# Order of the first loads and of deferred steps in a hybrid attention and recurrence layer

## The chip, the cores and the metric

The kernel runs on one core of a Trainium2 chip. The metric is the device time of one execution in microseconds (us), the median of several runs. Engines: PE is the matrix engine, DVE the vector engine, ACT the scalar engine, POOL the general engine; SP issues the DMAs. A matmul's stationary operand is loaded first (PEld).

## The reference

One layer of a mixer. Context tokens (128) and latent tokens (1024), 1152 in all, each of width 1024, are normalised and modulated; one input projection gives six parts of width 1024 (queries, keys, values, the attention's gate, the recurrence's input and gate). Eight heads of differential attention and a bidirectional gated linear recurrence read the same normalised input.

```python
h = rms_norm(x, g_pre) * (1.0 + scale) + shift      # shift, scale, gate = split(silu(cond) @ w_ada + b_ada)
q, k, v, g_att, x_lru, g_lru = split(h @ w_in)
a = softmax(q1 k1) - lam * softmax(q2 k2)            # 8 heads; latents see context and latents
att = rms_norm(a @ v, g_subln) * (1 - lam_init) * silu(g_att)
u = centred_conv(x_lru); hf, hb = forward and backward linear scans of gated u
lru = (hf + hb) * silu(g_lru)
y = x + gate * rms_norm(concat(att, lru) @ w_out, g_post)   # also out: context keys, values, last states
```

## The kernel before

Everything is issued by hand in program order: each engine works its own queue in that order, and an instruction that waits holds up all that stands behind it on its engine. Products are split into high and low halves, so each needs three matmuls (`mm3`, line 118).

**First stage (lines 365 to 595).** Loads go out on SP in the order of the string in line 379: `A`, `B`, `C`, `D` are the four 512-column parts of the modulation matrix, each in four tiles of 512 KB (ring `wa` of 8, line 372); `x0` to `x7` are the transposed input, 576 KB each; `w` is a 512 KB block of the input projection. `mod(part, b)` (line 430) multiplies one modulation tile on PE; `mod_rows` copies the finished row off PSUM on ACT; `mod_turn` transposes it on PE and adds the bias on DVE; `scales`, `bounds` and `unit_h` turn it into the scale and shift of four x tiles. A and B serve x0 to x3, C and D serve x4 to x7; C and D accumulate in the PSUM banks of A and B. `sqsum(k)` squares a tile on ACT and adds it on DVE; nine small matmuls (line 521) sum over partitions, Newton steps give the reciprocal root on DVE, nine matmuls (line 529) spread it into `rb`. `normed(k)` multiplies a tile by `rb` (DVE), `modulate(k)` scales and shifts it and makes the high half `hTh` (ACT, or DVE for 6 and 7), `h_lo(k)` makes the low half (DVE). `w_square`, `w_unit`, `w_hi`, `w_lo` do the same for a weight block: square on ACT, sum on PE, power of two on DVE, high half on ACT, low half on DVE. `first_chunk(k)` and the loop in line 590 are the first real projection, tile by tile.

**Recurrence and projections (lines 621 to 1135).** A chunk (line 356) is 24 matmuls over 384 tokens, for values over 128 tokens; three chunks are one block of 128 columns, nine are a pair of value blocks. After each chunk of the second part, `tick()` (line 351) runs steps that were put off by `after(d, step)`. PSUM banks for chunks come from a ring of five (`small`, line 255), which the small matmuls (`un`, `wu`, `vmt`, `vmu`, `ktp`) share. The order of blocks is queries 0, 1, values 0, keys 0, 1, then for each further pair queries, queries, keys, keys, values, then the last two attention gates. A query or key block (`qk_block`, line 891) has the steps `squares` (ACT, sum of squares), `power` (PE sum `un`, DVE power of two), `turned` (rotary, four DVE operations), `halves` (ACT high, DVE low) and `send` (SP). A value block (`v_block`, line 960) has `peak`, `spread` (PE and DVE), `halves` and `send`. The recurrence's last block has its rest put off in the same way (lines 862 to 871).

**Attention (from line 1138)** starts with loads of keys, queries, the first output weights (`load_wo`, split on ACT and DVE or POOL) and a tile of the recurrence's result (`load_lt`).

## Time and profile before

| | before |
|---|---|
| median of three runs | 1272.1 us (1271.8 to 1272.23) |
| the profiled execution, its own time | 1273.15 us |
| its span | 1271.4 us |
| busy PE / DVE / ACT / POOL, share of the span | 90% / 82% / 62% / 24% |
| mean granted clock of PE | 0.967 of full |
| bytes moved by DMA | 188.77 MB |

The span is what the trace covers; the execution's own time holds 1.75 us more. Shares of busy time are averages over stages with different limits, so each stage is read by itself: a list of waits names who was late, a timeline shows the order on one engine, and a table of stretches gives the clock that PE was granted.

### The profile page before, as it was taken

The numbers are of one execution on the slowest core, as the hardware profiler recorded it, in microseconds if no ns is written. First come the engines' busy times: TensorE is split into PE (matmuls) and PEld (weight loads), VectorE is DVE, ScalarE is ACT, GpSimd is POOL, SyncE is SP. The second block draws the span as 40 slices with busy tenths as digits, with TensorE's granted clock in tenths as the row PEclk, the third lists the DMA queues.
The fourth block names the chain that finished last, engine by engine and source line by source line (L and its number), as shares of the span: only waits on it lengthen the run. The fifth ranks groups of instructions, "written<-read, shape, count | busy, mean of one in ns | idle before, by whom it ended". The sixth has DMA issues, their size and how long they took to land.

```text
span 1271.4 us, 20656 instructions
## 1 busy us (share of the span) xinstructions
PE 1145.8 (90%) x7804; PEld 791.4 (62%) x7804; DVE 1037.2 (82%) x1880; ACT 787.8 (62%) x1330; POOL 300.1 (24%) x172
## 2 busy tenths in 40 slices
PE   4879999999999789999899979988989888989886
PEld 1246666666666656675766747665666666666665
DVE  5686898889887878878868548899898989999976
ACT  4447577657766445645445347777877786777632
POOL 0000000000000000000000013345955586557724
PEclk8899999999999889999899989999999999999998
DMA  9311312231223244534433276999887998888864
GB/s 364 134 42 43 114 62 78 90 114 62 78 90 104 89 121 140 141 125 133 142 125 90 58 255 134 211 200 226 187 210 179 230 213 178 200 203 215 199 208 153
DMA packets 277820, 188.77 MB, mean 148 GB/s; under 512 B 196172, under 2 KB 246092, under 8 KB 276952
## 3 DMA queue, kind: packets, MB, share of 16 engines
q1 hardware_dynamic: 277432, 186.60, 54.2%
q8 instruction: 61, 1.00, 0.3%
q10 hardware_dynamic: 288, 0.85, 0.2%
q14 instruction: 39, 0.32, 0.1%
HBM read 102.20 MB, written 46.94 MB: 117 GB/s over the span
## 4 chain that ended last, share of the span: by engine, by line
DVE 38%; PE 34%; ACT 12%; issue 6%; DMA 5%; POOL 3%; SPq 1%; DVEq 0%; ACTq 0%; POOLq 0%
DVE mx L1228 6%; DVE e L1256 4%; DVE wlo L323 2%; PE ga L119 2%; DMA t<-a 2%; PE ga L120 2%; PE s L1219 2%; PE ga L121 2%; PE s L1221 2%; POOL a L1260 2%; ACT e L1238 2%; PE v L119 2%; PE v L121 2%; PE v L120 2%; PE x L119 1%
## 5 line engine op out<-in xcount | busy, mean ns | idle before, releaser
L1238 ACT ACTIVATE e<-s,mx,back 128x1152 f32<-128x1152 f32 (+1 forms) x144 | 175.5, 1218 | 68.7 <-DVE fa L1246 19.0
L1260 POOL TENSOR_TENSOR a<-e,a 128x1152 f16<-128x1152 f32 (+1 forms) x72 | 157.9, 2193 | 173.2 <-ACT a L1259 164.9
L113 POOL TENSOR_TENSOR wol<-wor,woh 128x512 fp32r<-128x512 f32 x24 | 33.7, 1406 | 692.3 <-ACT woh L222 692.3
L1228 DVE TENSOR_REDUCE mx<-s 128x1 f32<-128x1152 f32 (+1 forms) x144 | 177.3, 1231 | 22.1 <-PE s L1221 21.3
L119 PEld LDWEIGHTS <-whi 128*128 128x128 f16 x960 | 97.4, 101 | 64.2 <-issue 7.8
L121 PEld LDWEIGHTS <-wlo 128*128 128x128 f16 x960 | 94.2, 98 | 67.3 <-issue 5.7
L120 PEld LDWEIGHTS <-whi 128*128 128x128 f16 x960 | 94.3, 98 | 59.2 <-issue 3.1
L1219 PE MATMUL s<-kt,qt 128*128 128x384 f16 (+1 forms) x400 | 89.9, 330 | 45.7 <-ACT e L1238 43.3
L1256 DVE SCALAR_TENSOR_TENSOR e<-e,fa,e 128x1152 f32<-128x1152 f32 (+1 forms) x72 | 115.2, 1601 | 7.1 <-POOL ot L1306 0.5
L119 PE MATMUL po<-woh,lt 128*128 128x512 f32 x216 | 99.4, 460 | 9.6 <-DMA lt<-mix 4.6
L119 PE MATMUL pv<-vt,t 128*128 128x128 f16 x584 | 103.5, 221 | 4.9 <-DMA t<-a 2.7
L120 PE MATMUL pv<-vt,t 128*128 128x128 f16 x584 | 103.0, 221 | 0.0
L121 PE MATMUL pv<-vt,t 128*128 128x128 f16 x584 | 102.9, 221 | 0.0
L1259 ACT CAST a<-e 128x1152 f16<-128x1152 f32 (+1 forms) x72 | 75.8, 1053 | 40.9 <-DVE e L1256 25.8
L1221 PE MATMUL s<-kt,qt 128*128 128x384 f16 (+1 forms) x400 | 89.3, 329 | 0.0
L121 PE MATMUL po<-woh,lt 128*128 128x512 f32 x216 | 87.3, 404 | 0.0
L120 PE MATMUL po<-wol,lt 128*128 128x512 f32 x216 | 87.1, 403 | 0.0
L119 PE MATMUL v<-whi,hTh 128*128 128x256 f16 x288 | 81.9, 284 | 4.5 <-ACT qfq L759 3.4
L120 PE MATMUL v<-wlo,hTh 128*128 128x256 f16 x288 | 81.9, 285 | 0.0
L121 PE MATMUL v<-whi,hTl 128*128 128x256 f16 x288 | 81.9, 284 | 0.0
L1219 PEld LDWEIGHTS <-qt 128*128 128x128 f16 x400 | 34.1, 99 | 75.9 <-issue 63.4
L323 DVE SCALAR_TENSOR_TENSOR wlo<-wraw,wboth,whi 128x512 f16<-128x512 f32 x94 | 66.3, 747 | 18.3 <-ACT whi L313 18.3
(361 smaller groups left out, 3245.3 us busy)
## 6 DMA issues: line engine op xcount, KB each, us to landing
wraw<-in_w_in_dram SPq DMA_DIRECT2D x48, 512.0 KB, 3.5
lt<-mix SPq DMA_DIRECT2D x27, 512.0 KB, 3.9
qs<-hlq SPq DMA_DIRECT2D x64, 144.0 KB, 2.6
qt<-qs SPq DMA_DIRECT2D x72, 128.0 KB, 3.3
wa<-in_w_ada_dram SPq DMA_DIRECT2D x16, 512.0 KB, 8.9
wor<-in_w_out_dram SPq DMA_DIRECT2D x32, 256.0 KB, 4.1
mix<-amo SPq DMA_DIRECT2D x6, 1152.0 KB, 5.8
vs<-v SPq DMA_DIRECT2D x8, 640.0 KB, 3.0
```

The costliest lines, as they stand in the source:

```text
L113: eng.tensor_tensor(out=lo, in0=val, in1=f(hi), op=ALU.subtract)
L119: PE.matmul(out, lhsT=lh, rhs=rh, start=start, stop=False)
L120: PE.matmul(out, lhsT=lh, rhs=rl, start=False, stop=False)
L121: PE.matmul(out, lhsT=ll, rhs=rh, start=False, stop=stop)
L323: V.scalar_tensor_tensor(out=lo[:, i % 2, r], in0=raws[i][:, r], scalar=wboth[:, i, x:x + 1], in1=hi[:, i % 2, r], op0=ALU.mult, op1=ALU.s ...
L1219: PE.matmul(sps[:, j, :w_], lhsT=qt[:, mp], rhs=kt_[:, mp, c], start=True, stop=False)
L1221: PE.matmul(sps[:, j, :w_], lhsT=qt[:, 2 + mp], rhs=kt_[:, mp, c], start=False, stop=True)
L1228: V.tensor_reduce(out=d["mx"][:, mp:mp + 1], in_=sv, axis=AX.XY, op=ALU.max, negate=True)
L1238: S.activation(out=e_[:, :nk].rearrange("p (j c) -> p j c", c=w_), in_=sv, func=AF.Exp, bias=d["mx"][:, mp:mp + 1], scale=unit, accum_out= ...
L1256: V.scalar_tensor_tensor(out=e1, in0=e1, scalar=d["fa"], in1=e0, op0=ALU.mult, op1=ALU.subtract)
L1259: S.copy(out=a16[:, 0:nk], in_=e1)
L1260: G.tensor_tensor(out=a16[:, nk:2 * nk], in0=e1, in1=a16[:, 0:nk], op=ALU.subtract)
```

## The change

The loads of the first stage are put in turns of two x tiles and one B tile, and the matmuls, sums and small steps of that stage follow that order; C and D are multiplied earlier in the program, and two weight-block squares move. In the projection stage the scratch output of `squares` is no longer a tile of the ring `a` but the one scratch tile `wjunk`, made wider; `power` stands ahead of `turned` and one chunk earlier; the value steps come two chunks later for the first pair and one chunk earlier for the others; the recurrence's rest starts its roots one chunk later and all that follows too. At the start of attention `load_lt(0, 0)` is issued ahead of the four `load_wo`.

```diff
--- before.py
+++ after.py
@@ -274,7 +274,7 @@
         place = {x: i for i, x in enumerate(order)}
         raws, wts = {}, {}
         cnt = {"load": 0, "square": 0, "unit": 0, "cast": 0, "tick": 0}
-        junk = wp.tile([P, KT, P], mybir.dt.bfloat16, name="wjunk", bufs=1)
+        junk = wp.tile([P, T + CTX], mybir.dt.bfloat16, name="wjunk", bufs=1)
 
         def w_load():
             i = cnt["load"]
@@ -287,7 +287,8 @@
 
         def w_square():
             i = cnt["square"]
-            S.activation(out=junk, in_=raws[i], func=AF.Square, accum_out=wsq[:, i:i + 1])
+            S.activation(out=junk[:, :D].rearrange("p (k c) -> p k c", k=KT), in_=raws[i], func=AF.Square,
+                         accum_out=wsq[:, i:i + 1])
             cnt["square"] += 1
 
         def w_unit(bank=None):
@@ -376,7 +377,7 @@
 
             xt = [sp.tile([P, T], F32, name=f"xt{k}") for k in range(KT)]
             what = {"A": (0, 1), "B": (0, 0), "C": (1, 1), "D": (1, 0)}
-            for x in "A0 A1 w A2 A3 B0 B1 x0 x1 x2 x3 x4 x5 x6 x7 B2 B3 C0 C1 C2 C3 D0 D1 D2 D3 w w w".split():
+            for x in "A0 A1 w A2 A3 x0 x1 B0 x2 x3 B1 x4 x5 B2 x6 x7 B3 C0 C1 C2 C3 D0 D1 D2 D3 w w w".split():
                 if x == "w":
                     w_load()
                 elif x[0] == "x":
@@ -508,56 +509,61 @@
             for b in range(4):
                 mod(*A, b)
             w_square()
+            mod(*B, 0)
             w_unit(ssq)
             w_lo(w_hi())
-            for b in range(2):
-                mod(*B, b)
-            for k in range(KT):
+            for k in range(3):
                 sqsum(k)
-                if k == 2:
-                    mod_rows(*A)
+            mod_rows(*A)
+            mod(*B, 1)
+            for k in range(3, 5):
+                sqsum(k)
             mod_turn(*A)
+            mod(*B, 2)
+            for k in range(5, KT):
+                sqsum(k)
+            mod(*B, 3)
+            mod_rows(*B)
+            mod(*C, 0)
+            mod_turn(*B)
+            scales(0)
+            bounds(0)
             for t in range(NT):
                 PE.matmul(ssq[:, t:t + 1], lhsT=qsum[:, t * P:(t + 1) * P], rhs=onesf[:, 0:1], start=True, stop=True)
             V.tensor_scalar(out=xc, in0=ssq[:, :NT], scalar1=-0.5 / D, scalar2=-0.5 * EPS, op0=ALU.mult, op1=ALU.add)
             for k in NEWTON:
                 newton(k, xc, yc, tcol)
-            for b in range(2, 4):
-                mod(*B, b)
-            mod_rows(*B)
+            mod(*C, 1)
+            unit_h(0)
+            mod(*C, 2)
             for t in range(NT):
                 PE.matmul(rb[:, t // 3, (t % 3) * P:(t % 3 + 1) * P], lhsT=yc[:, t:t + 1].to_broadcast([P, P]), rhs=ident,
                           start=True, stop=True)
-            mod_turn(*B)
             normed(0)
-            scales(0)
-            bounds(0)
-            unit_h(0)
-            for b in range(2):
-                mod(*C, b)
             normed(1)
             modulate(0, S)
+            mod(*C, 3)
             modulate(1, S)
             normed(2)
             h_lo(0)
+            mod_rows(*C)
             normed(3)
-            for b in range(2, 4):
-                mod(*C, b)
+            mod(*D_, 0)
             modulate(2, S)
-            mod_rows(*C)
+            h_lo(1)
+            mod_turn(*C)
+            for b in range(1, 4):
+                mod(*D_, b)
+            normed(4)
             modulate(3, S)
-            h_lo(1)
-            normed(4)
-            mod_turn(*C)
-            for b in range(4):
-                mod(*D_, b)
-            mod_rows(*D_)
             h_lo(2)
             normed(5)
+            w_square()
+            mod_rows(*D_)
             h_lo(3)
             normed(6)
+            w_unit(ssq)
             normed(7)
-            w_square()
             accs = [small(f"x0_{j}") for j in range(NCH)]
             accb = big("x0b")
 
@@ -574,8 +580,6 @@
             shares()
             for k in range(2, 4):
                 first_chunk(k)
-            w_unit(ssq)
-            w_square()
             modulate(4, S)
             modulate(6, hi=V)
             h_lo(6)
@@ -590,6 +594,7 @@
             for x, k in enumerate((4, 6, 7, 5)):
                 for j in range(NCH):
                     chunk(accb[:, j], 16, 0, j, [k], x == 0, x == 3)
+            w_square()
             w_back(w_unit(ssq))
             w_square()
             w_ahead(0, ssq)
@@ -863,12 +868,13 @@
         decays(p)
         gated(p, 0)
         gated(p, 1)
-        after(1, lambda: (weights(p, 0), weights(p, 1), roots(p)))
-        after(2, lambda: (driven(p, 0), scan(p, 0)))
-        after(3, lambda: (driven(p, 1), scan(p, 1)))
-        after(4, lambda: (both(p), mixed(p)))
-        after(5, lambda: (mix_split(p), finish_state()))
-        after(6, lambda: mix_send(p))
+        after(1, lambda: (weights(p, 0), weights(p, 1)))
+        after(2, lambda: roots(p))
+        after(3, lambda: (driven(p, 0), scan(p, 0)))
+        after(4, lambda: (driven(p, 1), scan(p, 1)))
+        after(5, lambda: (both(p), mixed(p)))
+        after(6, lambda: (mix_split(p), finish_state()))
+        after(7, lambda: mix_send(p))
 
 
         cosT = lp.tile([P, LAT], F32, tag="uh", name="cosT", bufs=1)
@@ -898,7 +904,6 @@
 
             def squares():
                 d["sq"] = lp.tile([P, 1], F32, tag="qsq", name=f"sq{name}")
-                junk = lp.tile([P, T + CTX], F32, tag="a", name=f"j{name}")
                 S.activation(out=junk[:, :w_], in_=t_[:, :w_], func=AF.Square, accum_out=d["sq"])
 
             def context_keys():
@@ -941,7 +946,7 @@
             if which:
                 nc.sync.dma_start(out=t_[:, T:], in_=io["cache_kT"][:, h])
 
-            steps = [squares, turned, power, halves, send]
+            steps = [squares, power, turned, halves, send]
             if not first:
                 for j in range(NCH):
                     qk_chunk(which, h, t_, j)
@@ -950,11 +955,11 @@
                 squares()
                 if which:
                     after(1, context_keys)
-                for x, step in zip((1, 2, 3, 4), steps[1:]):
+                for x, step in zip((1, 1, 3, 4), steps[1:]):
                     after(x, step)
             else:
 
-                for x, step in zip(((6, 8, 9, 10, 11), (7, 10, 11, 12, 13))[h], steps):
+                for x, step in zip(((5, 7, 8, 10, 11), (7, 9, 10, 12, 13))[h], steps):
                     after(x - 3 * h, step)
 
         def v_block(pr):
@@ -1023,10 +1028,8 @@
                     nc.sync.dma_start(out=vs[pr][:, m], in_=d["v16"][m])
 
             d = {}
-            after(2, peak)
-            after(3, spread)
-            after(4, halves)
-            after(5, send)
+            for x, step in zip((1, 2, 3, 4) if pr else (4, 5, 6, 7), (peak, spread, halves, send)):
+                after(x, step)
 
 
 
@@ -1117,9 +1120,9 @@
             load_k(0, n)
         for n in range(2):
             load_q(n)
+        load_lt(0, 0)
         for kt in GROUPS[0]:
             load_wo(kt, 0)
-        load_lt(0, 0)
         after(2, lambda: [split_wo(kt, 0, V if kt % 2 else G) for kt in GROUPS[0][:2]])
         after(3, lambda: [split_wo(kt, 0, V if kt % 2 else G) for kt in GROUPS[0][2:]])
         after(3, lambda: [load_wo(kt, 1) for kt in GROUPS[0]])
```

## Rows read from the trace of the kernel before

**Rows 1.** table of stretches (stretch, length, busy us per engine, granted clock, DMA share, GB/s): projections

```profile
390.00:740.00 350.00, 325.90 (x2253) 225.55 (x2250) 260.91 (x587) 168.62 (x295) 0.00 (x0) 0.96 0.40 122
```

**Rows 2.** timeline of the first 40 us (start, length, engine, line, operation, tiles, count, [idle before])

```profile
5.62 8.62 PE L433 MATMUL modpA<-wa,cs 128*2 128x512 f32 x16 [5.62 <-DVE sp L406]
...
18.62 10.13 DVE L505 TENSOR_TENSOR qsum<-qsum,sq 128x1152 f32<-128x1152 f32 x7 [0.82 <-ACT sq L503]
...
28.89 4.00 PE L521 MATMUL ssq<-onesf,qsum 128*128 128x1 f32 x18 [8.30 <-DVE modT L445]
...
32.82 5.24 PE L433 MATMUL modpB<-wa,cs 128*2 128x512 f32 x8
...
37.98 2.27 PE L529 MATMUL rb<-ident,yc 128*128 128x128 f32 x18
```

**Rows 3.** the x tiles: issue of their loads and time to landing

```profile
L384 SPq DMA_DIRECT2D xt<-in_xT_dram x8: 328/328/467, 5.1 to 13.6; - x8
...
DMA to landing us min/median/max: 9.8/11.1/11.4
```

**Rows 4.** table of stretches as in rows 1: two stretches of the first stage

```profile
16.00:20.00 4.00, 2.07 (x5) 0.26 (x3) 2.64 (x2) 4.00 (x5) 0.00 (x0) 1.00 1.02 411
...
24.00:28.00 4.00, 0.00 (x0) 0.00 (x0) 3.69 (x4) 2.44 (x3) 0.00 (x0) 0.50 1.05 388
```

**Rows 5.** timeline from 40 to 90 us

```profile
40.71 1.34 DVE L482 TENSOR_TENSOR xt<-xt,rb 128x1152 f32<-128x1152 f32 x1
...
44.47 1.63 ACT L491 ACTIVATE xt<-xt,sh,sc 128x128 f32<-128x128 f32 x2 [5.81 <-DVE sh L470]
...
52.62 0.57 ACT L438 COPY rows<-modpA 2x512 f32<-2x512 f32 x1
...
53.57 7.03 PE L433 MATMUL modpB<-wa,cs 128*2 128x512 f32 x16
...
64.00 0.17 DVE L445 TENSOR_TENSOR modT<-ssq,vec 128x8 f32<-128x8 f32 x1 [3.82 <-PE ssq L443]
...
66.56 1.62 ACT L491 ACTIVATE xt<-xt,sh,sc 128x128 f32<-128x128 f32 x2 [3.12 <-DVE sh L470]
```

**Rows 6.** timeline of DVE from 68 us

```profile
69.10 1.06 DVE L488 TENSOR_SCALAR xt<-xt,sc,sh 128x128 f32<-128x128 f32 x2
...
72.66 1.34 DVE L116 TENSOR_TENSOR hTl<-xt,hTh 128x1152 f16<-128x1152 f32 x1
```

**Rows 7.** waits of PE from 385 to 745 us (waiting, waited for: total, times, longest)

```profile
PE unk L913 <- ACT jk L902: 6.4, 2, 4.3
...
PE vmt L997 <- DVE vm L990: 5.3, 1, 5.3
PE po L119 <- DMA lt<-mix: 4.6, 1, 4.6
PE v L119 <- ACT qfq L759: 3.4, 1, 3.4
```

**Rows 8.** timeline of ACT: the first query block's squares

```profile
437.51 1.16 ACT L902 ACTIVATE jq<-qfq 128x1152 f32<-128x1152 f32 x1 [11.38 <-DMA mix<-lmh]
```

**Rows 9.** timeline of DVE: end of the recurrence's last split

```profile
434.01 1.36 DVE L113 TENSOR_TENSOR lml<-lsg,lmh 128x1152 fp32r<-128x1152 f32 x1
```

**Rows 10.** tables of stretches, one query chunk (PE, ACT) and one value chunk (PE, DVE, ACT)

```profile
500.72:504.61 3.89, 3.89 (x25) 0.58 (x1) 1.00 0.79 277
...
546.60:549.22 2.62, 2.62 (x25) 0.00 (x0) 0.60 (x3) 1.00 0.02 6
```

**Rows 11.** timeline of ACT: squares of key blocks 3 and 5

```profile
535.03 1.25 ACT L902 ACTIVATE jk<-qfk 128x1280 f32<-128x1280 f32 x1
...
616.22 1.25 ACT L902 ACTIVATE jk<-qfk 128x1280 f32<-128x1280 f32 x1
```

**Rows 12.** timelines of SP and ACT around the start of attention

```profile
733.63 0.82 SPq L229 DMA_DIRECT2D kt<-ks  x2
...
743.11 1.51 ACT L727 ACTIVATE sg<-ga,winv 128x384 f32<-128x384 f32 x3
```

## Prediction

> **What bounds the kernel now.** I read three views in this order: the table of stretches, the timeline of the first 90 us, and the waits of PE in the projection stage. From 390 to 740 us PE is busy 325.9 of 350 us and DVE only 260.9 [rows 1], so about 24 us of PE waits are all that the moved steps can win there, plus the slower matmuls that follow a long wait. The first stage is different. There PE is mostly waiting, and the end is set by a chain that goes round the engines: modulation tiles (PE), sums of squares (ACT and DVE, 18.62 to 28.75), partition sums (PE, 28.89 to 32.89), two B tiles (PE, to 38.06), the spread (PE, 37.98 to 40.25) [rows 2], then the first `normed` at 40.71, and, with the scales still to come, the first `modulate` at 44.47 [rows 5]. A second loop in it is C's row (ACT, 52.62), D's sixteen passes (PE, 53.57 to 60.6), D's turn (DVE, 64.00) and the modulation of x4 (ACT, 66.56) [rows 5]. After that the same work follows in the same order in both kernels, so a gain at x4 to x7 is carried to the end.
>
> **Part 1, the first loads and their order.** An x tile costs the queue (13.6 + 11.4 - 5.1 - 9.8) / 7 = 1.44 us and x0 lands at 5.1 + 9.8 = 14.9 [rows 3]; so 512 KB cost 1.28. B0 now lands with four A, one w and two x ahead of it, 64 KB more than x0 had to its end before: 15.1. PE is through with A at 14.2 [rows 2], waits 0.9, does B0 in 4 x 0.43 = 1.7 (sixteen passes of A and D take 7.03 to 8.6, 0.43 to 0.54 each [rows 2, 5]), and only then sums the first weight block, which the sums of x stand behind on ACT. That is 2.6 us of loss: the sums end at 28.75 + 2.65 + 0.1 (A's turn now in DVE's way) = 31.5. The last x lands at 25.0 + 1.3 and B3 at 27.6, both before that.
> Then the gain. Partition sums start at 31.5 and take 2.0, half of the 4.0 they took at half clock [rows 2, 4], an estimate; C1 1.7, the unit of h 0.5, C2 1.7, with the Newton steps on DVE beside them; the spread 2.27 [rows 2]. Sum: 31.5 + 2.0 + 1.7 + 0.5 + 1.7 + 2.3 = 39.7 for the first `normed`, only 1.0 sooner than 40.71. But the scales are done by then, so `modulate` starts one `normed` (1.34) later, at 41.1 against 44.47: 3.4 won. ACT needs (52.62 - 44.47) / 3 = 2.72 per tile [rows 5]; C's row is now behind two tiles instead of three: 41.1 + 5.4 = 46.5, done 47.1, against 53.2: 6.1 won. One D tile is done before that, so twelve passes are left; four of them at half clock after a pause, 0.86 x 4 + 0.43 x 8 = 6.9: 54.4 against 60.6. D's row, two first chunks (2.9) and the turn follow as before, and one weight sum (0.3) has come in between: modulation of x4 at 66.56 - 5.9 = 60.6. The DVE work for x6 stood 69.10 - 66.56 = 2.5 behind it [rows 5, 6], because a weight unit's sum on PE waited for two first chunks; that unit now comes earlier, so 0.95 remains: 61.5, 7.5 won. From there the order to the low half of x4 (72.66 to 74.0 [rows 6]) is unchanged. **Start: -7.5.** Its bounds: all twelve D passes at full clock give 1.7 more; partition sums and C tiles at half clock (4.0 + 2.7 + 0.5 + 1.7) take 3.0 away. So -4.5 to -9.2. On SP nothing waits longer: C and D want the slots of A and B, which are free sooner.
>
> [...] In 16 to 20 PE was busy 2.07 of 4 us and granted the full clock; in 24 to 28, with nothing to do, 0.50 [rows 4]. After the change PE has bursts of 1.7 us with pauses of 2 to 2.5 us in that place. [...]
>
> **Part 2, the recurrence's rest and the first values.** Before, three waits lie here: 3.4 (value chunk 2 wants a bank whose evacuation stands on ACT behind the roots), 5.3 (`unq`; its squares write a scratch tile of ring `a` and wait 11.38 on ACT for the mix DMA [rows 8]) and 5.3 (`vmt` waits for DVE) [rows 7]. The chunks behind them start at half clock, an estimated 1.5 to 2 each: 5 more, 19 in all. After: roots one chunk later let the middle bank go early, so the first wait is 0.7. The squares wait for no DMA, the scratch tile is ACT's alone; as a bf16 store of the same count it costs the same. But `unq` now stands two chunks earlier: its squares are through on ACT some 2.2 after PE gets there, and the ring of five gives its bank to value chunk 6, while DVE reads it only behind the recurrence's split, which ends at 435.4 [rows 9] and now at some 436: another 4.6, and 1.5 of clock behind it. On SP the mix send goes one chunk later, with a weight block's load behind it that nobody waits for yet. `vmt` stands behind two more chunks and waits for nothing. 19 - 9 = 10 won by the end of the second key block's first chunk. Queued behind the value halves (ACT 2.6) are now the key halves and the squares of key block 1, so its `unk` waits 2.0 and a bank 1.0 to 1.3: 3.3 lost. **-6.7**, bounds -10 (no bank wait is that long) and -2 (both waits for `unq` add up and the clock stays low).
>
> **Part 3, `power` one chunk earlier.** It adds nothing to do, but PE now comes to `un` one chunk sooner, and all chunks behind it wait if the squares aren't there. The squares of a block stand on ACT behind the halves of the block before it, these behind that block's rotary steps on DVE, so the round of ACT and DVE sets their time, not PE. In the query blocks they were through about when the next block's first chunk ended, so nothing is lost. At key blocks 3 and 5 they ended at 536.4 and 617.6 [rows 11] and PE already waited 2.0 and 4.3 (6.4 in sum [rows 7]); there PE arrives one value chunk, 2.62 [rows 10], sooner and does that chunk after the wait instead of before. Price 2.4 and 2.6; key block 7, at which `unk` waited for nothing, 0.8. The value halves of pairs 1 to 3 come one chunk earlier and take DVE's 3 us out of a crowded block: 0.4 back. **+5.4**, bounds 0 and +9 (one query chunk, 3.9 [rows 10], in one group more).
>
> **Part 4, the start of attention.** The last value block is sent one chunk sooner, ahead of the gate's send on SP. The loads of keys waited for that send until 733.63 [rows 12]; they can start some 3 sooner, and the output weights come one 512 KB load (1.3) later behind `load_lt`. ACT casts those weights ahead of the last gate's sigmoid (743.11 [rows 12]), whose bank the first output matmul needs, the wait of 4.6 [rows 7]. 3.5 - 1.2 = 2.3 won. **-2.3**, bounds 0 (keys wait for the gate's tile) and -3.5.
>
> **The sum** is -7.5 - 6.7 + 5.4 - 2.3 = -11.1. The profiled execution took 1273.15 with a span of 1271.4, 1.05 above the median of 1272.1. After: 1262.0 for such an execution, 1261.0 for the median.
>
> **Rivals.** (a) *The early `power` costs nothing*: the round of ACT and DVE keeps ahead, since it enters key block 2 earlier. For it speaks that query blocks show no wait at all; against it the two squares of rows 11, which depend on that round alone. Then part 3 is 0, and the 3.3 of part 2 falls away: 1261.0 - 5.4 - 3.3 = 1252.3. Chance 0.15. (b) *Low clock in the first stage* from the sums to C2: start -4.5 or less, or part 2 at its poor bound: 1264 to 1267.5. For it the 0.50 of 24 to 28, against it the 1.00 of 16 to 20 [rows 4]. Chance 0.20. [...] Chance 0.05. (d) *It doesn't do what it says*: PE's early B0 keeps the sums late, low clock eats half the start, and part 3 takes its dearer end: 1270 to 1274. Chance 0.06.
>
> **How the numbers follow.** Forecast 0.54, with 1257 to 1264.5 as its own range. Time 1261. A range that leaves out no more than 0.2 reaches from a little below (a) to the slow end of (b): 1251 to 1268. A measurement here tells 0.2%, 2.5 us, from no change. Faster holds the forecast, (a) and nearly all of (b): 0.88; same 0.06; slower 0.06.
>
> **What would show it.** `qsum` ending near 31.5 and the first `modulate` near 41 (right), or beyond 44 with the clock at 0.50 (wrong). DVE's work for x6 starting near 61.5. No wait of a square on the mix DMA, no wait of `vmt`; new waits of PE for `unq` and for the bank of value chunk 6 of 2 to 5 us. Waits of `unk` for squares at key blocks 1, 3 and 5 of some 2, 3.5 and 5.5 us: if they are absent, (a) holds. The first output matmul 2 us sooner after the last gate chunk. The forecast is wrong if the loads land in another order, or if the DVE work of the recurrence's rest meets the value chunks later than read here.

## The result and the profile after

The kernel before takes 1272.2 us and the changed one 1255.5 (ratio 0.9856, interval 0.9814 to 0.9897): 16.6 us less. The forecast was 11.1 us less, 1261.0, with a range from 1251 to 1268. The profiled execution of the changed kernel took 1255.92 with a span of 1254.1, against 1273.15 and 1271.4.

**The first stage.** The changed kernel's table of stretches (columns as in [rows 1]) answers [rows 4]:

```profile
32.00:36.00 4.00, 4.00 (x21) 2.39 (x22) 2.16 (x15) 0.00 (x0) 0.00 (x0) 0.76 1.05 386
36.00:40.00 4.00, 4.00 (x11) 0.89 (x10) 1.50 (x9) 0.00 (x0) 0.00 (x0) 0.82 1.04 404
...
44.00:48.00 4.00, 1.47 (x4) 0.17 (x2) 3.65 (x4) 3.94 (x5) 0.00 (x0) 0.96 0.00 0
48.00:52.00 4.00, 2.58 (x7) 0.84 (x8) 3.53 (x4) 3.97 (x6) 0.17 (x3) 0.50 0.00 0
52.00:56.00 4.00, 4.00 (x7) 0.64 (x6) 3.80 (x3) 3.81 (x6) 0.17 (x3) 0.68 0.00 0
...
68.00:72.00 4.00, 2.54 (x9) 1.16 (x9) 3.93 (x6) 3.94 (x7) 0.00 (x0) 0.52 0.00 0
```

Its timeline of PE, then ACT and DVE, answers [rows 2, 5, 6]:

```profile
31.96 2.17 PE L532 MATMUL ssq<-onesf,qsum 128*128 128x1 f32 x18 [0.26 <-DVE modT L446]
34.06 3.56 PE L434 MATMUL modpA<-wa,cs 128*2 128x512 f32 x4
...
37.86 1.88 PE L434 MATMUL modpA<-wa,cs 128*2 128x512 f32 x4
39.67 2.27 PE L540 MATMUL rb<-ident,yc 128*128 128x128 f32 x18
...
49.42 0.58 PE L444 MATMUL ssq<-ident,rows 2*128 2x2 f32 x4 [3.95 <-ACT rows L439]
49.93 7.58 PE L434 MATMUL modpB<-wa,cs 128*2 128x512 f32 x12
...
69.46 0.48 PE L120 MATMUL x0b<-hTl,whi 128*128 128x384 f16 x1 [2.58 <-DVE hTl L116]
```

```profile
43.37 1.63 ACT L492 ACTIVATE xt<-xt,sh,sc 128x128 f32<-128x128 f32 x2 [13.11 <-DVE xt L483]
48.80 0.57 ACT L439 COPY rows<-modpA 2x512 f32<-2x512 f32 x1
63.70 1.63 ACT L492 ACTIVATE xt<-xt,sh,sc 128x128 f32<-128x128 f32 x2 [5.57 <-DVE sh L471]
...
41.98 3.88 DVE L483 TENSOR_TENSOR xt<-xt,rb 128x1152 f32<-128x1152 f32 x3 [2.89 <-PE rb L540]
64.50 1.06 DVE L489 TENSOR_SCALAR xt<-xt,sc,sh 128x128 f32<-128x128 f32 x2
```

The partition sums take 2.17 (forecast 2.0), but the second C tile behind them takes 3.56 where the third takes 1.88: 34.06 to 37.55 was granted 0.51, the sums ahead of it and the third tile 1.00. So `normed` starts at 41.98 and not at 39.7, and everything to x4 hangs on that. D's twelve passes take 7.58 (0.63 each) where sixteen took 7.03 before [rows 5]: PE had waited 3.95 us in front of them, and the stretch from 48 to 52 was granted 0.50. PE also waits 1.1 and 2.6 us ahead of the last first-block chunks (x0b), and their stretch, 68 to 72, is granted 0.52.

**The projections.** The waits of PE from 385 to 745 answer [rows 7]:

```profile
PE unk L918 <- ACT wjunk L907: 9.8, 3, 4.3
PE po L119 <- DVE sg L738: 7.1, 1, 7.1
PE k L119 <- DVE wunit L194: 4.6, 3, 1.7
PE unq L918 <- ACT wjunk L907: 2.5, 4, 1.6
PE v L119 <- DVE qksc L194: 2.3, 1, 2.3
...
PE v L119 <- ACT qfq L764: 0.8, 1, 0.8
```

The waits for `jq` and `vmt` are gone, as forecast; `unk` waits longer (9.8 against 6.4), and there is a line that the forecast has only once, key chunks waiting for a weight unit (4.6, three times).

**Three marks** carry the rest, all read from timelines. *Q* is where PE is done with the last of the gate chunks that alternate with query chunks, *G* the end of the last gate chunk of all, *X* the first transpose (SP) of attention. From X on the instructions are the same in all kernels here. X for the two kernels, each in two executions (before, before again, changed, changed again):

```profile
759.02 1.29 SPq L1262 DMA_TRANSPOSE t<-a  x1
```

```profile
758.49 1.29 SPq L1262 DMA_TRANSPOSE t<-a  x1
```

```profile
748.39 1.28 SPq L1265 DMA_TRANSPOSE t<-a  x1
```

```profile
749.11 1.31 SPq L1265 DMA_TRANSPOSE t<-a  x1
```

All kernels of this study, in us (last column: profiled time less X):

| kernel | Q | Q to G | G to X | X | profiled | median | ratio to before, interval | from X |
|---|---|---|---|---|---|---|---|---|
| before | 400.4 | 338.7 | 20.0 | 759.0 | 1273.2 | 1272.2 | | 514.1 |
| b0_before_again | 400.4 | 338.9 | 19.2 | 758.5 | 1270.6 | 1272.8 | 0.9997, 0.9984 to 1.0010 | 512.1 |
| changed | 397.1 | 333.2 | 18.0 | 748.4 | 1255.9 | 1255.5 | 0.9856, 0.9814 to 0.9897 | 507.5 |
| e0_again | 397.7 | 333.3 | 18.1 | 749.1 | 1260.5 | 1255.3 | 0.9869, 0.9849 to 0.9889 | 511.4 |
| e1_first_stage | 397.9 | 337.1 | 19.6 | 754.5 | 1266.9 | 1266.6 | 0.9943, 0.9924 to 0.9962 | 512.3 |
| e2_projection | 400.8 | 332.0 | 16.5 | 749.4 | 1256.6 | 1256.8 | 0.9872, 0.9850 to 0.9895 | 507.3 |
| e3_latent_first | 402.7 | 339.0 | 21.5 | 763.1 | 1273.6 | 1274.3 | 1.0009, 0.9991 to 1.0026 | 510.4 |
| e4_scratch | 400.6 | 332.5 | 19.4 | 752.5 | 1260.5 | 1261.6 | 0.9912, 0.9892 to 0.9932 | 508.0 |
| e5_power_late | 396.3 | 324.7 | 18.3 | 739.3 | 1251.3 | 1248.0 | 0.9800, 0.9768 to 0.9832 | 512.0 |
| e6_weights_first | 396.8 | 333.3 | 15.4 | 745.5 | 1256.3 | 1254.8 | 0.9856, 0.9832 to 0.9880 | 510.8 |
| e8_spread_early | 392.2 | 332.1 | 17.8 | 742.1 | 1250.2 | 1252.9 | 0.9844, 0.9819 to 0.9869 | 508.1 |
| e9_filler | 392.9 | 332.9 | 17.5 | 743.3 | 1253.0 | 1252.6 | 0.9834, 0.9814 to 0.9854 | 509.7 |
| f0_three | 392.7 | 325.5 | 15.5 | 733.8 | 1243.5 | 1241.5 | 0.9748, 0.9726 to 0.9771 | 509.7 |
| f1_turns | 394.1 | 323.9 | 16.3 | 734.2 | 1245.8 | 1245.3 | 0.9788, 0.9766 to 0.9809 | 511.6 |

A ratio is to the runs of before on the same chip, whose medians lay between 1272.2 and 1274.1. At Q, G and X the two executions of before, and the two of changed, agree within 1 us; from X on they differ by up to 4. Over the five executions that have the old first stage (before twice, e2, e3, e4) Q spreads from 400.4 to 402.7, over the five with the new one unedited (changed twice, e1, e5, e6) from 396.3 to 397.9. So an edit ahead of attention is read from the marks, and the medians say what it is worth as a whole.

### The profile page after: what moved, and what is told of

It is laid out like the page before. It is cut to its first block, busy times and chain, and to the rows that moved or that the text cites. A ratio compares the mean times of both kernels' runs of the same rounds, so it can differ in the third digit from the quotient of the medians.

```text
span 1254.1 us, 20667 instructions
## 1 busy us (share of the span) xinstructions
PE 1141.9 (91%) x7804; PEld 786.2 (63%) x7804; DVE 1033.5 (82%) x1880; ACT 786.9 (63%) x1330; POOL 302.1 (24%) x172
## 4 chain that ended last, share of the span: by engine, by line
DVE 36%; PE 36%; ACT 10%; DMA 7%; issue 7%; POOL 3%; SPq 1%; DVEq 0%; ACTq 0%; POOLq 0%
DVE mx L1231 6%; DVE e L1259 5%; DVE wlo L324 3%; PE s L1222 2%; PE s L1224 2%; PE ga L119 2%; POOL a L1263 2%; PE v L119 2%; PE v L120 2%; PE v L121 2%; PE ga L120 2%; PE ga L121 2%; ACT e L1241 2%; PE po L119 2%; PE po L120 1%
## 5 line engine op out<-in xcount | busy, mean ns | idle before, releaser
L1222 PE MATMUL s<-kt,qt 128*128 128x384 f16 (+1 forms) x400 | 88.0, 324 | 42.4 <-ACT e L1241 40.4
L1224 PE MATMUL s<-kt,qt 128*128 128x384 f16 (+1 forms) x400 | 87.8, 325 | 0.0
## 6 DMA issues: line engine op xcount, KB each, us to landing
wraw<-in_w_in_dram SPq DMA_DIRECT2D x48, 512.0 KB, 3.6
lt<-mix SPq DMA_DIRECT2D x27, 512.0 KB, 4.1
wa<-in_w_ada_dram SPq DMA_DIRECT2D x16, 512.0 KB, 10.6
```

The lines of the kernel that those rows point to most:

```text
L1222: PE.matmul(sps[:, j, :w_], lhsT=qt[:, mp], rhs=kt_[:, mp, c], start=True, stop=False)
L1224: PE.matmul(sps[:, j, :w_], lhsT=qt[:, 2 + mp], rhs=kt_[:, mp, c], start=False, stop=True)
```

## The experiments

**e1_first_stage**: the kernel before with the hunks of the first stage alone.

```diff
-            for x in "A0 A1 w A2 A3 B0 B1 x0 x1 x2 x3 x4 x5 x6 x7 B2 B3 C0 ...
+            for x in "A0 A1 w A2 A3 x0 x1 B0 x2 x3 B1 x4 x5 B2 x6 x7 B3 C0 ...
 ...  (with it the changed order from the second A tile to the first block's chunks)
```

> The kernel before with the first stage of the change alone: its order of first loads, its order of work up to the first query block, its places for the weight sums; everything from the recurrence on stays as before. Theory T (read from the two traces): the first query block starts 3.2 to 3.4 us sooner than before (forecast of the record: 7.5), low clock having taken the rest, and the last gate chunk of the projection also ends 3.4 sooner, since nothing in between is changed; PE's waits for unq and vmt are there as before. Theory R (the forecast was right about the first stage, and the rest of the change undoes part of it): 7.5 sooner at the first query block. On the whole: the attention stage, whose instructions are the same in both kernels, took 6.7 us less in the changed kernel. If that is tied to the moved steps or to the order of loads at its start, this kernel takes 1272.2 - 3.4 = 1268.8. If any kernel that reaches it at another time than before gets it, 1262 to 1263.

Measured: Q 2.5 sooner, where T expected 3.2 to 3.4 and R 7.5. R falls. G comes 4.1 to 4.4 sooner, a little more than T has it. The median is 6.7 below before's; 3.9 to 4.5 of that stand at X.

**e2_projection**: the kernel before with the scratch tile, the recurrence's later rest, and the new chunks of the power and value steps.

```diff
-        after(1, lambda: (weights(p, 0), weights(p, 1), roots(p)))
-        after(2, lambda: (driven(p, 0), scan(p, 0)))
+        after(1, lambda: (weights(p, 0), weights(p, 1)))
+        after(2, lambda: roots(p))
 ...
-                junk = lp.tile([P, T + CTX], F32, tag="a", name=f"j{name}")
 ...
-            steps = [squares, turned, power, halves, send]
+            steps = [squares, power, turned, halves, send]
 ...
-            after(2, peak)
+            for x, step in zip((1, 2, 3, 4) if pr else (4, 5, 6, 7), (peak, spread, halves, send)):
```

> The kernel before with the moved steps of the projection alone: scratch tile of the squares, the recurrence's rest one chunk later, the value steps and the power-of-two step on other chunks. The first stage and the order of loads at the start of attention stay as before. Theory T (from the two traces): 0 at the first query block, 13.2 us sooner than before when key block 1's first chunk ends, 9.9 at the end of the third query block, 5.3 at the last gate chunk, the difference lost at waits of unk; po, the first output matmul of attention, waits for the latent load as before. Theory R (the forecast's sizes): 10.0, 6.7 and 1.3. On the whole 1272.2 - 5.3 = 1266.9, or 1260 if the attention stage also gives its 6.7.

Measured: 9.5 sooner than before at the end of the third and fourth query block (T 9.9, R 6.7) and 6.2 to 6.5 sooner at G (T 5.3, R 1.3); T is near, R too low. `po` waits 2.9, and not for the latent load but for the last gate's `sg`.

**e4_scratch**: of these, the scratch tile alone.

```diff
-                junk = lp.tile([P, T + CTX], F32, tag="a", name=f"j{name}")
                 S.activation(out=junk[:, :w_], in_=t_[:, :w_], func=AF.Square, accum_out=d["sq"])
```

> The kernel before with one change: the squares of query and key blocks write the scratch tile of the weight squares and no longer a tile of ring a, so they do not wait for the transfer of mix. The forecast priced the three waits at the entry of the values (3.4 for a bank, 5.3 for unq, 5.3 for vmt, about 5 of slow matmuls behind them) together. Theory T: the wait of unq alone goes, and the slow chunk behind it: 5.3 to 7 us sooner at the value chunk behind unq, and vmt, whose peak DVE has to work out from the same value chunks, comes as much sooner: 5.3 to 7 at the end of key block 1's first chunk, 4 to 6 at the last gate chunk. Theory R: DVE sets the time of vmt, whenever the chunks come; its wait of 5.26 grows by what unq gives, and at key block 1 nothing is left: 0 to 1. The rest of the 13.2 that the moved steps won there (3.4 for the bank and 5.3 for vmt) is then the later roots' and the later peak's alone, or needs all of them together.

Measured: the squares of the first query block, at 437.51 behind a wait of 11.38 for the transfer of `mix` [rows 8], now run without one, in 1.16 as before though the store is bf16:

```profile
426.20 1.16 ACT L902 ACTIVATE wjunk<-qfq 128x1152 bf16<-128x1152 f32 x1
```

The value block that they stand in takes 29.4 us, 7.3 less. Of that, `vmt` and a key chunk take back some 3; waits of PE:

```profile
PE vmt L997 <- DVE vm L990: 6.2, 1, 6.2
...
PE k L119 <- ACT vf L978: 1.1, 1, 1.1
```

At the end of key block 1's first chunk 4.0 are left (T 5.3 to 7, R 0 to 1), and 6.0 at G (T 4 to 6). T is near, though `vmt` gives back part of the gain as R has it; R's size falls. The scratch tile by itself is worth as much from Q to G (332.5) as all of e2 together (332.0).

**e5_power_late**: the changed kernel with `power` on its old chunk in all blocks but query blocks 0 and 1 (these keep the change's `power`, two chunks earlier than before).

```diff
-                for x, step in zip((1, 1, 3, 4), steps[1:]):
+                for x, step in zip((1, 2, 3, 4), (turned, power, halves, send)):
```

> The changed kernel, with the power-of-two step of query and key blocks (from the third query block and the first key block of the second pair on) back where it was: one chunk later and behind the rotary step. Theory T (the forecast's part 3): the early step costs, since PE waits for unk 4.28 us at value block 1 and 4.08 at value block 2; with it one value chunk (2.8 us) later these waits are 1.5 and 1.3 and the matmul after them faster, and the last gate chunk ends 4.5 to 6 us sooner than in the changed kernel (730.35). Rival (a) of the record (the early step costs nothing, the losses belong to DVE and ACT being behind, wherever the step stands): within 1 us of 730.35. On the whole 1250 to 1251 or 1255.5, if the attention stage takes as long as in the changed kernel.

Measured: G at 720.99, 9.4 sooner; 8.6 of it between Q and G. More than T's 4.5 to 6, and (a) is refuted. Where it lies, from the ends of the blocks on PE (us per group):

| | v0 | k0,1 | q2,3 | k2,3 | v1 | q4,5 | k4,5 | v2 | q6,7 | k6,7 | v3 | gate |
|---|---|---|---|---|---|---|---|---|---|---|---|---|
| before | 36.7 | 31.8 | 24.1 | 24.1 | 28.4 | 24.2 | 26.4 | 31.5 | 24.2 | 26.1 | 25.7 | 23.8 |
| changed | 31.1 | 25.5 | 25.9 | 24.2 | 31.6 | 24.7 | 27.2 | 30.7 | 24.7 | 27.0 | 24.9 | 23.8 |
| e5_power_late | 31.5 | 24.4 | 24.1 | 24.1 | 29.2 | 24.2 | 25.1 | 32.0 | 24.2 | 24.8 | 25.7 | 23.8 |

The early step costs 2.4 at v1, which the forecast had, gains 1.2 at v2 and 0.8 at v3, and costs 1.1 and 1.8 at k0,1 and q2,3, 2.1 and 2.2 at the two later pairs of key blocks, and 0.5 at each of the later query pairs. PE in the changed kernel, between two chunks of key block 5, shows where the key blocks lose it:

```profile
588.77 0.28 PE L297 MATMUL wu<-wsq,onesf 128*128 128x1 f32 x2
588.91 0.31 PE L911 MATMUL ktp<-ident,qfk 128*128 128x128 f32 x1
589.15 0.38 PE L918 MATMUL unk<-sqk,onesf 128*128 128x1 f32 x2
591.28 0.32 PE L119 MATMUL k<-hTh,whi 128*128 128x384 f16 x1 [1.75 <-DVE wunit L194]
```

The chunk before and three small results take a bank each of the ring of five, and the next chunk waits for DVE to read `wu`. Three alone do not do it: at key block 3 of the same kernel they stand in the same place, and the chunk follows at once:

```profile
507.38 0.28 PE L297 MATMUL wu<-wsq,onesf 128*128 128x1 f32 x2
507.52 0.31 PE L911 MATMUL ktp<-ident,qfk 128*128 128x128 f32 x1
507.66 0.28 PE L918 MATMUL unk<-sqk,onesf 128*128 128x1 f32 x2
507.80 0.32 PE L119 MATMUL k<-hTh,whi 128*128 128x384 f16 x1
```

Where the chunk waits, a fifth bank is taken: by a partial sum of the output gate (`gacc`, at 584.26 and 671.06) at key blocks 5 and 7 and by `vmt` (455.82) at key block 1. That the ring is then full is worked out from the order of the matmuls and fits all four places; no run isolates it. With the step late only two small results stand there, and at key block 5 the chunk follows at once:

```profile
582.22 0.28 PE L297 MATMUL wu<-wsq,onesf 128*128 128x1 f32 x2
582.36 0.31 PE L911 MATMUL ktp<-ident,qfk 128*128 128x128 f32 x1
582.50 0.33 PE L119 MATMUL k<-hTh,whi 128*128 128x384 f16 x1
```

**e3_latent_first**: the kernel before with the latent tile ahead of the output weights; **e6_weights_first**: the changed kernel with the old order.

```diff
+        load_lt(0, 0)
         for kt in GROUPS[0]:
             load_wo(kt, 0)
-        load_lt(0, 0)
```

> The kernel before with one change: at the start of attention the first latent tile is loaded ahead of the four output weight blocks. The forecast: before, po waits 4.59 us for that latent load; with it gone, the wait is 1.2 for the output weights' casts, and since the loads of keys do not come sooner here, scores and transposes start at most 1 us sooner: 1271 to 1272. Theory T: po waits for the last gate's sigmoid instead (7.05 us in the changed kernel, of which the earlier arrival of PE explains none), so po starts within 1 us of before, and the first transpose as well: 1272. Theory A: this order of loads sets how the transfers of the attention stage fall against each other, and that stage is 6.7 us shorter in the changed kernel because of it: 1265 to 1266.

> The changed kernel with the first latent tile loaded behind the four output weight blocks again, as it was before. The forecast (part 4): without the swap po waits for the latent load, some 1 to 2 us longer than with it; po at 738.5 to 740 where the changed kernel has 737.5. Theory T (from the traces): in the changed kernel po waits 7.05 us for the last gate's sigmoid, which stands on ACT behind casts of output weights, and those wait for the weights' load; with the weights first the casts come 2 to 3.5 us sooner, as in the kernel with the moved projection steps alone (there po waited 2.90), and po starts at 734 to 735.5; first transpose at 745 to 746.5, on the whole 2 to 3 us less than the changed kernel, inside its spread.

Measured: in e3 `po` comes 3.8 after G (before 4.9), but the first transpose 21.5 after it (before 19.2 and 20.0). Its first query block stood 2.3 later although nothing ahead of it is edited, so only distances from G are read. In e6 `po` starts at 734.13 and the transposes at 745.5, 15.4 after G, against 18.0 in the changed kernel: as T had it, and the forecast (`po` later than 737.5) falls. The same both ways: the swap costs 1.5 to 2.3 us up to X in e3 and 2.7 in e6. ACT, changed kernel:

```profile
730.51 1.32 ACT L222 CAST woh<-wor 128x512 fp32r<-128x512 f32 x2 [10.14 <-DMA wor<-in_w_out_dram]
733.37 1.30 ACT L222 CAST woh<-wor 128x512 fp32r<-128x512 f32 x2 [1.54 <-DMA wor<-in_w_out_dram]
734.58 1.51 ACT L732 ACTIVATE sg<-ga,winv 128x384 f32<-128x384 f32 x3
```

and e6:

```profile
728.30 0.62 ACT L222 CAST woh<-wor 128x512 fp32r<-128x512 f32 x1 [8.14 <-DMA wor<-in_w_out_dram]
729.16 1.95 ACT L222 CAST woh<-wor 128x512 fp32r<-128x512 f32 x3 [0.25 <-DMA wor<-in_w_out_dram]
731.02 1.52 ACT L732 ACTIVATE sg<-ga,winv 128x384 f32<-128x384 f32 x3
```

The sigmoid stands on ACT behind four casts that wait for the weights' load; 3.6 us sooner with the weights first. The first transpose does not hang on `po`, which in e3 comes sooner while the transpose comes later. DVE, changed kernel:

```profile
739.65 1.20 DVE L113 TENSOR_TENSOR wol<-wor,woh 128x512 fp32r<-128x512 f32 x1 [1.15 <-ACT woh L222]
740.77 0.28 DVE L1231 TENSOR_REDUCE mx<-s 128x1 f32<-128x128 f32 x1
```

The maximum over the first scores (`mx`) stands on DVE behind the low half of the eighth weight block, which waits for its cast and so for its load. It comes 11.4 after G in before, 12.9 in e3, 10.4 in the changed kernel and 7.8 in e6, and X 8.6, 8.6, 7.6 and 7.6 behind it. The medians of changed and e6 differ by 0.5 to 0.7, less than their spread.

**e9_filler**: the changed kernel with matmuls that nobody reads in two of PE's pauses.

```diff
+            def busy(n):
+                for _ in range(n):
+                    PE.matmul(ssq[:, 64:192], lhsT=onesf, rhs=ident, start=True, stop=True)
 ...
             h_lo(1)
+            busy(14)
             mod_turn(*C)
 ...
+            busy(17)
             for x, k in enumerate((4, 6, 7, 5)):
```

> The changed kernel with matmuls that nobody reads added on PE in two of its pauses of the first stage: 14 of 128 columns between the first D tile and C's turn (PE waits 3.95 us there for ACT's row), 17 ahead of the last first-block chunks (x0b, where it waits 1.1 and 2.6 us for DVE). The output is unaffected. Theory T: the level that the chip grants follows what PE did just before. With the pauses filled, D's twelve passes take 5.2 to 5.8 us instead of 7.58 and the 24 first matmuls of x0b 5.3 instead of 6.8 (the 0.50 of the stretch from 48 to 52 goes to near 1); D's row then comes when ACT's squares are through (1.7 sooner) and the first query block 2.4 to 2.9 sooner than in the changed kernel. Rival R: D's passes and x0b's chunks wait for something else, and the level has nothing to do with the pauses: no gain, or a loss of up to 2 from the added matmuls in PE's way.

Measured, table of stretches and PE:

```profile
44.00:48.00 4.00, 4.00 (x28) 2.96 (x27) 3.65 (x4) 3.94 (x5) 0.00 (x0) 1.00 0.00 1
48.00:52.00 4.00, 3.37 (x15) 1.16 (x14) 3.42 (x5) 3.97 (x6) 0.17 (x3) 1.00 0.00 0
...
68.00:72.00 4.00, 3.92 (x25) 2.26 (x24) 3.93 (x5) 2.83 (x6) 0.00 (x0) 1.00 0.00 0
```

```profile
45.13 3.39 PE L439 MATMUL ssq<-ident,onesf 128*128 128x128 f32 x28
...
49.49 5.31 PE L434 MATMUL modpB<-wa,cs 128*2 128x512 f32 x12
```

The same twelve passes take 5.31 in place of 7.58, at 1.00 in place of 0.50 and 0.68. Q comes 4.3 sooner, above T's 2.4 to 2.9, since x0b's chunks, from 67.27 and granted 1.00 (68 to 72), gain more than forecast (24 matmuls behind the first 4.3 in place of 6.8). R falls. For D's passes the pause is shown to be the cause: nothing else ahead of them was edited, the added work makes PE busier, and over all runs their time goes with the wait ahead of them: 5.31 behind 0.63 (e9) and 1.44 (before, the last twelve of sixteen), 6.95 and 6.98 behind 2.24 (f0, e8), 7.58 to 8.04 behind 3.95 (changed twice, e1, e5, e6). For x0b it is not shown: e8 and f0 have the same waits of 1.1 and 2.6 ahead of it, unfilled, and 4.3 for the 24 as well.

**e8_spread_early**: the changed kernel with the spread of the root ahead of the third C tile.

```diff
-            mod(*C, 1)
             unit_h(0)
-            mod(*C, 2)
+            mod(*C, 1)
             for t in range(NT):
                 PE.matmul(rb[:, t // 3, ...
+            mod(*C, 2)
```

> The changed kernel with the third C tile behind the spread of the root (rb) and the unit of h ahead of the second C tile. In the changed kernel the Newton steps end at 36.6, but the spread starts only at 39.67, since the second C tile ran at the low level (3.56 us for four passes) and the unit and the third C tile stand before it. Theory T: the spread starts at 38.0, the first normed at 40.3 instead of 41.98, the first modulation on ACT at 41.7 instead of 43.37, and the whole first stage ends 1.5 to 1.7 sooner (first query block). Rival: the spread or the third C tile, now behind a pause-free stretch of small matmuls, runs at the low level too and gives it back, or D's row is bound by the passes of D, not by the modulation: 0 to 0.5 at the first query block.

Measured: the spread starts at 38.02, as T has it, though here the slow tile was the last B tile (3.57) and no longer the C tile. Q comes 4.9 sooner, not 1.5 to 1.7: PE waited only 2.24 us ahead of D's passes, which took 6.98, and x0b's 24 matmuls took 4.3, which T did not foresee. So this edit's own price isn't parted from that of these two bursts.

**e0_again** and **b0_before_again**: nothing edited.

> The changed kernel itself once more, nothing edited. Five executions of programs whose attention stage holds the same instructions took 507.2 to 514.2 us from the first transpose to the end, and the kernel before, in its three profiled forms with the old first stage, reached the first query block up to 2.3 us apart. Theory T: what the changed kernel won beyond the first transpose (6.7 us) is the spread of the attention stage from execution to execution and no property of the change; then this execution takes 508 to 514 from the first transpose and may well differ from the first by some us, while first query block, last gate chunk and first transpose stand within 2 us of 381, 730.4 and 748.4. Theory A: it is a property of the changed kernel (how its transfers meet), and this execution again takes 507 to 508.

> The kernel before once more, nothing edited. So far ten profiled executions took 507.2 to 514.2 us from the first transpose to the end, the one of before the longest (514.2), and the old first stage put the last gate chunk of the recurrence's part up to 2.3 us apart. Theory T: both are spread from execution to execution. Then this one takes 508 to 513 from the first transpose (mean of the ten: 510.6), and its first query block may be 0 to 2.5 later than in the first profile. Theory A: a long attention stage belongs to the kernel before: 513 to 515 again.

Measured: 511.4 from X for the changed kernel (first 507.5) and 512.1 for before (first 514.1). Both times theory T's range holds: the 6.6 us by which the first two executions differ there are 0.7 between the second two, while Q, G and X come again within 1 us. The slow tile moved too: in e0 the second C tile takes 1.88, and the last B tile in front of the sums 3.57:

```profile
27.55 3.57 PE L434 MATMUL modpB<-wa,cs 128*2 128x512 f32 x4 [1.74 <-DMA wa<-in_w_ada_dram]
...
35.68 1.88 PE L434 MATMUL modpA<-wa,cs 128*2 128x512 f32 x4
...
39.61 2.27 PE L540 MATMUL rb<-ident,yc 128*128 128x128 f32 x18
```

The spread starts at 39.61, against 39.67: one slow tile on the path in both. It is not always there. In e5, whose program is the same up to Q, neither tile is slow (the second C tile 1.88):

```profile
34.23 1.88 PE L434 MATMUL modpA<-wa,cs 128*2 128x512 f32 x4
...
38.16 2.27 PE L540 MATMUL rb<-ident,yc 128*128 128x128 f32 x18
```

The spread starts 1.5 sooner there, and Q is 0.8 sooner than in the first execution of the changed kernel (396.3), since D's passes took 8.04.

**f0_three** and **f1_turns**: e5, e6 and e8 in one; then D's tiles and row earlier, and 12 unread matmuls ahead of x0b.

```diff
+            for b in range(4):
+                mod(*D_, b)
             modulate(2, S)
             h_lo(1)
+            mod_rows(*D_)
             mod_turn(*C)
             normed(4)
 ...
```

> The changed kernel with three edits together that each stood alone so far: the power-of-two step back on its later chunk, the output weights ahead of the first latent tile, the spread of the root ahead of the third C tile. If they add: last gate chunk 9.2 + 6.0 sooner than in the changed kernel (730.4), that is 715 to 717, po 3 sooner still than that, first transpose at 729 to 732 (748.4 in the changed kernel), on the whole 1255.4 - 7.5 - 0.6 - 2.5 = 1244.8 by the medians of the three, 1238 to 1241 by the first transposes and a mean attention stage of 510.3. If the attention stage takes back what comes earlier (its own transfers set its end), 1246 to 1250.

> The last kernel, with D's four tiles one after another ahead of C's turn, D's row on ACT ahead of the fourth modulation, D's turn and the scales ahead of the first chunks, and 12 matmuls that nobody reads in the pause before the last first-block chunks (their results enter nothing). Theory T (low clock and the order on ACT set the end of the first stage): D's sixteen passes take 7.5 us without a pause behind them, D's row is done near 52 instead of 58, the modulation of x4 starts near 56 instead of 61 to 64, then DVE, busy since the first normed, is the bound: the first stage ends 2 to 3.5 sooner than in the last kernel, and the whole with it. Rival: DVE is the bound already, since its sixteen large steps to x3 and the scales now come one behind the other; 0 to 1 sooner.

Measured: f0 takes 1241.5, 14 below the changed kernel and some 32 below before. Its G, 718.2, and X, 733.8, are 1 to 2 later than expected: the edits nearly add, and the attention stage takes nothing back. f1 loses: D's row is done at 52.6 and x4's modulation starts at 57.5, near what theory T had, but Q comes 1.4 later than in f0. DVE waits 2.42 for C's turn, which now stands behind D's passes, with four `normed` behind it; and ahead of the first `normed` the second C tile took 3.57 and the spread 3.05, against 1.88 and 2.27 in f0. Its rival (0 to 1 sooner) was nearer, though it missed too.

## Why the prediction was right, point by point

The stated range held (the forecast's own narrower one, 1257 to 1264.5, did not), and up to the first transpose so did the sum: the mean of two executions each is 10.0 sooner there (758.8, 748.8), forecast 11.1. But its terms were off by more than the sum. That they add up is luck: the 4.5 that the start fell short and the 4.2 that the projections won beyond the forecast cancel.

- **Start, -7.5: measured -3.0** (Q 400.4 and 400.4 against 397.1 and 397.7; -3.5 between the medians of the five executions that each first stage has), outside its bounds of -4.5 to -9.2. Loads, sums of x and partition sums came as worked out (B0 at 15.12 for 15.1, qsum done near 31.5, sums 2.17 for 2.0). The step that failed is the full clock for the bursts of this stage, in three places. At one C tile ahead of `normed` (0.51) it is 1.8 us (41.98 for 39.7, the rest a later start of the sums); it stays in the first modulation (43.37 for 41.1) and C's row (done 49.4 for 47.1). D's passes (0.50 and 0.68) took 0.7 more than 6.9, so x4 came at 63.70 for 60.6, and DVE's work for x6 at 64.50 for 61.5, 4.6 sooner than before. Then x0b (0.52) gave 1.2 of that back: its 24 matmuls behind the wait took 6.8 where before took 5.6, so "a gain at x4 to x7 is carried to the end" failed too. The C tile alone does not explain it: in e5 it took 1.88, `normed` started at 40.47, and Q was still only 4.0 sooner than before, with 8.04 for D's passes and 7.0 for x0b's 24. The low bound priced low clock once, at the sums and C; in e9, where both later places are granted 1.00, Q comes 4.3 sooner. So the low clock of rival (b) is there in this stage; its place and its time are not as (b) has them.
- **Clock and bursts.** The row that I went by, 1.00 from 16 to 20 [rows 4], holds no burst behind a pause: in before PE is busy 12.44 of 12.44 us from 5.62 to 18.06, granted 1.00, and the 2.07 us of that row are its end. After 8.30 us of waiting the partition sums got 0.50 there (28.89 to 32.8) and took 4.00 [rows 2]. In e9 filling a pause of 3.95 us turns 0.50 into 1.00 behind it, and 7.58 into 5.31. For a low clock that lasts through the whole first stage, to which the forecast gave 0.05, no run shows a case: the changed kernel was granted 1.00 for the sums, the third C tile and the spread.
- **Part 2, -6.7: measured -10.0 and -10.3** from Q to the end of q2,3 (changed less before, two executions each), at its bound of -10. Most of the mechanism stood: no wait on the mix transfer, none of `vmt`, new waits of 0.8, 1.6 and 2.3 (forecast 0.7, about 2 and 4.6) for `qfq`, `unq` and a bank. The size that failed is what these leave: the forecast had 10 won at the end of key block 1's first chunk, the traces show 13.4 and 13.7, because the waits are 4.7 where it put 7.5. The slow matmuls behind them came as it had them: behind the wait of 2.3 sixteen at 0.21 us apart, where the others are 0.11, which is 1.6 more (forecast 1.5). In before it is 1.6, 1.4 and 1.9 behind the three waits (forecast 5 in all), with 0.50 granted from 438.82 to 442.3. The wait for the bank alone was 2.3 short: DVE's split kept its place (end at 432.5, 2.8 ahead of before's 435.4 [rows 9], about what the start had won), but PE came to it later than worked out. The 3.3 lost behind that came as forecast (3.4: a bank 1.1, `unk` 1.5), but not as the value halves' doing: with `power` late, k0,1 and q2,3 give 3.0 of it back, so it belongs to the early `power`, as rival (a) counts it. e4 prices the scratch tile by itself at 6 from Q to G; how later roots and later value steps share the rest was not parted.
- **Part 3, +5.4: measured +4.5 and +4.6** from the end of q2,3 to G. e5, which moves `power` back and nothing else, prices the early step at 8.6 from Q to G, against 8.7 (5.4 and the 3.3 of part 2); without it the other moved steps win 14.1 (e5 less the mean of before). So the sign is shown, and rival (a) is refuted. The size is right by luck, for the list behind it was wrong: of 2.4, 2.6 and 0.8 only the first came. "In the query blocks nothing is lost" is nearly so (three waits for `unq` of 0.3; the 1.8 at q2,3 is key block 1's `unk`). The dearest part, 2.1 and 2.2 in the key blocks, is no wait for squares at all but a bank of the ring. I followed the squares on ACT and did not count the small results that stand between two chunks.
- **Part 4, -2.3: measured -1.5** from G to X. The keys' loads did come some 3 us sooner against G. But "the output weights come one load later" was priced at 1.2 and cost 2.7 (18.0 against e6's 15.4): the sigmoid waits for four casts, so for the last of four loads, and the scores' maximum for the eighth. The path was wrong as well: the first output matmul was to come 2 us sooner after the last gate chunk and came 2.2 to 2.4 later (`po` waits 7.1 where it waited 4.6 [rows 7]), while the first transpose hangs on that maximum. The swap itself was a loss.
- **Attention, 0: by the medians some -7.** The medians differ by 16.6 (17.5 in the second pair of runs), and 10.0 of that is there at X. In the profiled executions the stage differs by 6.6 in the first pair and 0.7 in the second. That the stage of one program spreads by some us is shown (514.1 and 512.1 in before, 507.5 and 511.4 in the changed kernel). Whether an edit has a part in it is open: the four executions with the old projection steps (before twice, e1, e3) took 510.4 to 514.1 from X, the ten others 507.3 to 512.0, so the groups overlap, but their means are 2.6 apart, and no run isolates a cause.

What happened is then: 3.0 at the start (forecast 7.5), 5.5 in the projections (14.1 less 8.6; forecast 1.3), 1.5 at the start of attention (forecast 2.3), and 6.6 in attention that no step has. The forecast was 5.5 too high: these 6.6, less the 1.1 by which its sum overshot.

## What to carry to other kernels

Count a moved step by every bank and queue slot that it holds at its new place, not only by the operand it waits for: here the one-column result of each block, one chunk earlier, cost 8.6 us in all, more than the change's first stage won. Look for waits that exist only because two things share a buffer: a scratch tile of its own gave 6 us up to G, with no step moved. Where PE works in bursts with pauses of some us, price every burst behind a pause at both levels, as here 5.31 and 7.58 for D's twelve passes, and try filling the pause before reordering around it.

## What was unexpected in the hardware

- Which burst is slow differs between executions of the same instructions. Behind 2.17 us of eighteen one-column matmuls the second C tile took 3.54 to 3.56 in three executions (changed, e6, e9) and 1.88 in three (e0, e1, e5); where it was fast, a B tile ahead of the sums was slow (3.57 in e0 and e1, 3.31 in e5), as one was in the changed kernel too (3.57 at 23.55).
- Twelve passes of 128x512 took 5.31 behind waits of PE of up to 1.44 us, 6.95 and 6.98 behind 2.24, and 7.58 to 8.04 behind 3.95. At x0b the wait does not tell: 24 matmuls took 6.8 to 7.0 behind 1.1 and 2.6 us in five executions and 4.3 behind the same two waits in e8 and f0, and 5.6 to 5.9 behind 1.0 and 4.3 with the old first stage. Filling the two pauses of the changed kernel gave 4.3 us at Q.
- The attention stage, the same instructions each time, took 507.3 to 514.1 us.
